# Feed-forward of an encoder trunk: eight of 22 gate/up pairs by seven block products, in a written order

## The chip, the cores and the metric

The kernel runs on one core of a Trainium2 chip. The metric is the device time of one execution in microseconds (us). TensorE multiplies, VectorE, ScalarE and POOL (GpSimd) work on tiles in SBUF, SP issues the transfers, and each engine takes its instructions in the order in which they stand in the program.

## The reference, cut to what matters

```python
D_MODEL, SEQ, DEPTH, D_FF = 1024, 512, 2, 2816          # everything float32

def swiglu(x, w_in, w_out):
    gate, up = jnp.split(x @ w_in, 2, axis=-1)
    return (jax.nn.silu(gate) * up) @ w_out

def reference(x, ffn_w_in, ffn_w_out, ln_g, ln_b, ...):
    for i in range(DEPTH):
        x = layer_norm(DN_ALPHA * x + 0.5 * swiglu(x, ffn_w_in[i, 0], ffn_w_out[i, 0]), ln_g[i, 0], ln_b[i, 0])
        m = neighbourhood_attention(x, ...) if i == 0 else rwkv7_bidir(x, ...)
        x = layer_norm(DN_ALPHA * x + m, ln_g[i, 1], ln_b[i, 1])
        x = layer_norm(DN_ALPHA * x + 0.5 * swiglu(x, ffn_w_in[i, 1], ffn_w_out[i, 1]), ln_g[i, 2], ln_b[i, 2])
    return x
```

There are four feed-forwards (`swiglu`), two in each layer. The change lies in them; the two token mixers stay as they are.

## The kernel before

Tokens: 512. D = 1024 is eight chunks of 128 rows, FF = 2816 is 22 blocks f of 128 columns. TensorE works in a float32 form with a short mantissa, so every operand is split in a high part (`split`, line 276, a copy on ScalarE) and a low part (line 277, raw minus high, on POOL or VectorE), and every product is three matmuls, high·high, high·low and low·high (`mm3`, lines 286 to 288).

`ffn()` runs in 11 steps c of two blocks f. For each f it loads the gate's and the up's weights (two tiles of 128x1024, 512 KB each, `load_cols`), splits them (low on POOL), and multiplies each with the tokens: 24 matmuls of 512 columns into one PSUM bank. Silu of the gate (ScalarE, L491) times the up product (VectorE, L493) gives a 128x512 block, which is stored as two token halves, so that each step has four quarter blocks (2 blocks by 2 halves) of 256.

The product with `w_out` is made by a seven-product scheme of its own (class `Winograd`), with the products X, Y, Z, V and, after the steps, a second Y and so on. `sums(c)` loads 1 MB of `w_out` (tile `ra`), makes sums of its four blocks, stores two of them in DRAM (`d_late`) and splits three (`wx`). Lines 498 to 501 make the sums on the token side; three of the seven quarter tiles are split in `an` and used at once, four in a ring tile (`keep`) for later. `early(c)` is 18 matmuls for X, Y and Z of step c (`product`, L923), issued one step later, so that a step has 96 + 18 = 114 matmuls. X, Y and Z hold six of the eight PSUM banks.

After the steps comes the tail: `add("V", ...)` loads weights in pairs of steps c, splits them (low half on POOL and on VectorE in turn) and multiplies them with the kept halves; `early(10)` stands in its midst; then twelve updates `more` (L520: x ← x + bank, on VectorE) empty the banks of X, Y and Z, and Y, Z and Y again follow with weights from `d_late` and `w_out`, the layer norm, and the next stage's first products (`lead`).

The order on the engines is a planner's: it places instructions by their dependences and by priorities. Inside `manual_schedule` the order in the code holds.

Of the kernel before, what the change touches and what calls it, by code (L numbers as in the profile page):

```python
# [10 lines left out]
F32 = mybir.dt.float32  # L11
# [7 lines left out]
P = 128  # L19
# [62 lines left out]
GN_EPS = 64e-5  # L82

# [22 lines left out]
class Trunk:  # L106
# [161 lines left out]
    def load_cols(self, w, c0, ring=False):  # L268
        return self.load_unit(w[c0 // P], None, ring)
# [191 lines left out]
    def ffn(self, xT, w_in, w_out, ln, nxt, lead=None):  # L461
# [8 lines left out]
        params = ln and self.ln_params(ln)  # L470
        out = Winograd(self, w_out)
        with self.pool("fa") as pool:
            out.pool = pool
            keep = [self.ring().rearrange("p (i n s) -> p i n s", i=2, n=4) for _ in range(npairs)]
            for c in range(npairs):
                if c == 2 and not params:
                    with self.behind(self.asked):
                        params = self.ln_params(ln)
                with self.behind(*() if c or ln else (self.asked,)):
                    out.sums(c)  # L480
                raw = pool.tile([P, 8, 256], F32, name="ar", tag="ar", bufs=1)
                for j in range(2):
                    f = 2 * c + j
                    if f == 0:
                        pps = self.follow()
                    elif not pps:
                        us = self.units if f == 1 else [self.load_cols(w_in, FF * i + f * P) for i in range(2)]
                        pps = [self.proj_cols(u, xT) for u in us]
                    pg, pu = pps.pop(0), pps.pop(0)
                    s = self.tmp()  # L490
                    nc.scalar.activation(s, pg, AF.Silu)  # L491

                    nc.vector.scalar_tensor_tensor(raw[:, 3:7:3] if j else raw[:, 0:8:7], halves_of(pu), 0.5, halves_of(s),  # L493
                                                   ALU.mult, ALU.mult)
                    if j == 0 and c:
                        out.early(c - 1)
                a = lambda n: raw[:, n]
                nc.vector.tensor_tensor(a(1), a(7), a(6), ALU.add)
                nc.vector.tensor_tensor(a(2), a(1), a(0), ALU.subtract)  # L499
                nc.gpsimd.tensor_tensor(a(4), a(0), a(7), ALU.subtract)  # L500
                nc.gpsimd.tensor_tensor(a(5), a(3), a(2), ALU.subtract)
                out.now[c] = pool.tile([P, 2, 3, 256], F32R, name="an", tag="an", bufs=1)
                self.split(out.now[c][:, 0], out.now[c][:, 1], raw[:, 0:3])
                self.split(keep[c][:, 0], keep[c][:, 1], raw[:, 3:7])
            out.keep = keep
# [3 lines left out]
            out.early(npairs - 1)  # L509
            out.add("V", 0, out.b21, range(late, npairs))  # L510
        nxt = nxt()
        with self.pool("fo") as pool:
            out.pool = pool
            out.begin(out.t3)
            fin = self.residual_norm(params, nxt)
# [20 lines left out]
            out.add("Y", 1, out.t3, range(npairs))  # L536
# [3 lines left out]
            out.add("Z", 2, out.b22, range(npairs), lag=8)  # L540
# [337 lines left out]

class Winograd:
# [8 lines left out]
    def sums(self, c):  # L888
# [3 lines left out]
        nc.sync.dma_start(r.rearrange("p j l f -> p j (l f)"), self.w[:, c])  # L892
        t3 = self.pool.tile([P, 512], F32, name="ts", tag="ts", bufs=1)
# [4 lines left out]
        nc.sync.dma_start(self.late[:, 0, c], t3)  # L898
# [1007 lines left out]
```

## Time and profile before

| | |
|---|---|
| time, median of 3 runs | 2162.34 us (2162.04 to 2162.39) |
| the profiled execution: time, span | 2161.41 us, 2159.6 us |
| clock granted to TensorE, mean | 0.999 of full speed |
| busy, share of the span: TensorE, VectorE, ScalarE, POOL | 99%, 49%, 44%, 65% |
| moved by DMA | 322 MB, 149 GB/s |
| the four feed-forwards, from the span's start | about 18 to 355, 600 to 950, 950 to 1290, 1800 to 2155 us |

The rows of the trace say: start, duration, engine, line, operation, tiles out<-in, shape, and in brackets the idle time ahead and what ended it. Groups say: count, busy time in all, mean ns of one, idle time ahead and what ended it. A chain row says start, duration, and what TensorE or a transfer did. A matmul's duration is modelled with its way through the array; what it costs in a stream is the distance of the starts.

### The profile page before, as it was taken

The page shows a single profiled execution, that of the slowest core. Times are in us where ns is not written, and L with a number is a line of the kernel's source. Part 1 is how long each engine was busy: PE and PEld are TensorE (multiplying, and loading weights), DVE is VectorE, ACT ScalarE, POOL GpSimd, SP SyncE. Part 2 cuts the span into 40 slices and gives each one's busy share as a digit, 9 for nine tenths or more (in the row PEclk, how much of TensorE's full clock was granted, in tenths as well). Part 3 has the DMA queues.
Part 4 walks back from the last instruction along what each step waited for, and adds up shares of the span by engine and source line. Part 5 has one row for each costly group of instructions (what it writes and reads, how often), then busy time and mean ns, then how long its engine had stood idle before and what let it go on. Part 6 is the DMA issues. An engine that isn't in the chain of part 4 may idle for free.

```text
span 2159.6 us, 35350 instructions
## 1 busy us (share of the span) xinstructions
PE 2134.2 (99%) x13952; PEld 1684.7 (78%) x13952; DVE 1059.7 (49%) x1526; ACT 954.2 (44%) x1675; POOL 1395.3 (65%) x1226
## 2 busy tenths in 40 slices
PE   9999999999999999999999999999999999999998
PEld 8888888888788888888888888445777558888876
DVE  3233355277333333653333369735998554333345
ACT  4333345367433333443333343636888433333333
POOL 5978855465378888568888653044788615877753
PEclk9999999999999999999999999999999999999999
DMA  7444462342244444634444543864454552444443
GB/s 214 150 152 140 148 230 93 113 122 84 88 156 142 141 142 142 224 132 137 142 141 142 188 143 123 284 223 123 124 138 130 177 190 92 143 141 142 137 165 127
DMA packets 146518, 322.00 MB, mean 149 GB/s; under 512 B 31184, under 2 KB 51280, under 8 KB 146352
## 3 DMA queue, kind: packets, MB, share of 16 engines
q1 hardware_dynamic: 146352, 319.74, 45.4%
q8 instruction: 110, 1.80, 0.4%
q14 instruction: 56, 0.46, 0.1%
HBM read 262.01 MB, written 45.61 MB: 142 GB/s over the span
## 4 chain that ended last, share of the span: by engine, by line
PE 94%; DVE 2%; DMA 1%; ACT 1%; issue 1%; SPq 0%; POOL 0%; DVEq 0%; ACTq 0%; POOLq 0%
PE bank L923 18%; PE bank L287 17%; PE bank L286 17%; PE bank L288 17%; PE a L1115 5%; PE bank L349 4%; PE g L1441 2%; PE y L1115 1%; PE bank L1308 1%; PE m L1115 1%; PE bank L677 1%; PE y L1618 1%; PE c L1611 1%; PE g L1115 1%; PE y L1641 1%
## 5 line engine op out<-in xcount | busy, mean ns | idle before, releaser
L277 POOL TENSOR_TENSOR w<-raw,w 128x1024 fp32r<-128x1024 f32 x198 | 484.6, 2449 | 228.5 <-ACT w L276 221.0
L286 PE MATMUL bank<-xT,w 128*128 128x512 f32 x1264 | 493.4, 390 | 0.0
L287 PE MATMUL bank<-xT,w 128*128 128x512 f32 x1264 | 492.3, 389 | 0.0
L288 PE MATMUL bank<-xT,w 128*128 128x512 f32 x1264 | 491.8, 389 | 0.0
L276 ACT ACTIVATE w<-raw 128x1024 fp32r<-128x1024 f32 x202 | 213.0, 1058 | 321.5 <-POOL ts L894 131.0
L493 DVE SCALAR_TENSOR_TENSOR ar<-bank,tmp 128x512 f32<-128x512 f32 x88 | 60.9, 692 | 572.1 <-PE bank L288 562.1
L288 PEld LDWEIGHTS bank<-xT,w 128*128 128x128 f32 x1264 | 237.3, 188 | 49.4
L286 PEld LDWEIGHTS bank<-xT,w 128*128 128x128 f32 x1264 | 237.3, 188 | 48.7
L287 PEld LDWEIGHTS bank<-xT,w 128*128 128x128 f32 x1264 | 237.4, 188 | 48.6
L923 PE MATMUL bank<-wx,an 128*128 128x512 f32 x792 | 187.5, 389 | 0.0
L923 PEld LDWEIGHTS bank<-wx,an 128*128 128x128 f32 x792 | 148.7, 188 | 31.2
L923 PE MATMUL bank<-w,ring 128*128 128x512 f32 x720 | 168.5, 390 | 1.7 <-POOL w L277 1.7
L277 POOL TENSOR_TENSOR wx<-ra,wx 128x512 fp32r<-128x512 f32 x132 | 167.0, 1292 | 3.2 <-ACT wx L276 3.2
L277 DVE TENSOR_TENSOR ring<-ar,ring 128x1024 fp32r<-128x1024 f32 x44 | 126.0, 2864 | 81.0 <-ACT ring L276 81.0
L923 PEld LDWEIGHTS bank<-w,ring 128*128 128x128 f32 x720 | 135.1, 188 | 30.6 <-POOL w L277 2.2
L491 ACT ACTIVATE tmp<-bank 128x512 f32<-128x512 f32 x88 | 52.6, 597 | 231.7 <-PE bank L288 231.6
L1550 POOL TENSOR_TENSOR tm<-qs,zs 128x126 f32<-128x126 f32 (+22 forms) x248 | 108.8, 439 | 62.8 <-DVE qs L1543 24.6
L1552 POOL TENSOR_TENSOR zs<-zs,tm 128x126 f32<-128x126 f32 (+22 forms) x248 | 109.0, 440 | 19.4
L276 ACT ACTIVATE wx<-ra 128x512 fp32r<-128x512 f32 x132 | 82.8, 633 | 77.0 <-PE bank L923 66.6
L277 POOL TENSOR_TENSOR ring<-raw,ring 128x1024 fp32r<-128x1024 f32 x24 | 59.9, 2508 | 74.8 <-ACT ring L276 74.8
L499 DVE TENSOR_TENSOR ar<-ar 128x256 f32<-128x256 f32 x44 | 92.5, 2102 | 1.5
L277 POOL TENSOR_TENSOR w<-xT,w 128x1024 fp32r<-128x1024 f32 x25 | 63.4, 2538 | 42.2 <-ACT w L276 42.2
(346 smaller groups left out, 3943.1 us busy)
## 6 DMA issues: line engine op xcount, KB each, us to landing
raw<-in_ffn_w_in_dram SPq DMA_DIRECT2D x176, 512.0 KB, 3.5
ra<-in_ffn_w_out_dram SPq DMA_DIRECT2D x44, 1024.0 KB, 5.0
xT<-d_late SPq DMA_DIRECT2D x29, 512.0 KB, 5.3
xT<-in_ffn_w_out_dram SPq DMA_DIRECT2D x23, 512.0 KB, 4.5
d_late<-ts SPq DMA_DIRECT2D x44, 256.0 KB, 3.0
d_late<-ra SPq DMA_DIRECT2D x44, 256.0 KB, 2.0
raw<-in_w_qkv_dram SPq DMA_DIRECT2D x16, 512.0 KB, 3.6
raw<-in_ffn_w_out_dram SPq DMA_DIRECT2D x12, 512.0 KB, 3.6
```

Source lines behind the costliest of these rows:

```text
L276: self.hi = self.nc.scalar.activation(h, raw, AF.Copy).ins
L277: self.lo = (eng or self.nc.vector).tensor_tensor(l, raw, h.bitcast(F32), ALU.subtract).ins
L286: nc.tensor.matmul(out, wh, xh, start=start, stop=False)
L287: nc.tensor.matmul(out, wh, xl, start=False, stop=False)
L288: nc.tensor.matmul(out, wl, xh, start=False, stop=stop)
L349: nc.tensor.matmul(acc[t, h], a, u[:, i, h * 512 : (h + 1) * 512], start=first and n == 0, stop=last and n == 2)
L493: nc.vector.scalar_tensor_tensor(raw[:, 3:7:3] if j else raw[:, 0:8:7], halves_of(pu), 0.5, halves_of(s), ALU.mult, ALU.mult)
L499: nc.vector.tensor_tensor(a(2), a(1), a(0), ALU.subtract)
L923: self.nc.tensor.matmul(acc, lhs, u[:, i], start=bool(first) and m == 0, stop=last and m == 2, skip_group_check=more)
L1115: self.nc.tensor.matmul(out[hs], w[:, hs], x, start=start, stop=stop)
L1550: nc.gpsimd.tensor_tensor(tv, qs[:, s, 0:s].rearrange("p (a o) -> p a o", o=1).broadcast_to([P, s, n]), zs[:, s : s + 1, c0:].broadcast_to ...
L1552: nc.gpsimd.tensor_tensor(zs[:, 0:s, c0:], zs[:, 0:s, c0:], tv, ALU.add)
```

## The change

For odd f from 7 to 21 (`SEVEN`, eight of 22, one in each step from the fourth, called a slot below) gate and up together are made as a 2x2 block product in the manner of Strassen and Winograd: rows gate and up, inner dimension in two halves of 512, tokens in two halves of 256. That takes seven products of 4 chunks x 3 = 12 matmuls of 256 columns (84) in place of 48 of 512 columns. The even f of those steps stay plain, with weights as half tiles.

- Weights come in half tiles of 128x512 (256 KB each). Four of them are turned into sums in place on VectorE (L1034, L1035, L1038, L1042), and eleven are split per slot; `weights()` is the thread that does so. L1042 is the last reader of the first raw half tile, which the next load then fills.
- The token side's four mixed tiles (128x1024) are made once per feed-forward, in the first two steps (`mixes`, L949 to L955, on VectorE).
- Only two PSUM banks serve a slot: the seven products are gathered through copies on ScalarE (L1076) and sums on VectorE (L1099, L1103, L1105, L1109).
- The order on TensorE, ScalarE and VectorE in slots is the string `FF_SEQ`: g is the plain f, s the seven products, e the 18 matmuls of the step before, w the weights, k the work behind the step before (`posts`), z and u the sums and splits of `w_out`.
- Weight splits of the plain blocks, the four sums on `ra`, and all the token sums move from POOL to VectorE.
- Of `keep`, two of four quarter tiles per step go to DRAM (`d_away`) and are read back for Z and the second Y (`recall`). The load of the norm's parameters stands behind the first Y.
- The first two weights of V are loaded and split inside the last slot (`opening`).

What stands in rows, at three places. In names of tiles the number is a running one; `w`, `wl2` are split weights, `xT_...` with a raw weight in it is a buffer that serves for loads in the tail, `ring` in the tail the kept halves, `bank` PSUM, `x0` to `x3` the residual.

First the tail of the first feed-forward. VectorE before: `w_2187` and `w_2237` are weights of V, the first updates follow.

```order
L277 TENSOR_TENSOR w_2187<-xT_2131,w_2187 128x1024 [waits DMAHW7_49,Activation_49]
L277 TENSOR_TENSOR ring_268<-ar_1977,ring_268 128x1024 [waits Activation_49]
L277 TENSOR_TENSOR w_2237<-xT_2132,w_2237 128x512 [waits DMAHW5_49,Activation_49]
L520 SCALAR_TENSOR_TENSOR x0_88<-x0_88,bank_491 128x512 [waits PE_49]
L520 SCALAR_TENSOR_TENSOR x1_89<-x1_89,bank_492 128x512 [waits DMAHW1_49,PE_49]
L520 SCALAR_TENSOR_TENSOR x2_90<-x2_90,bank_499 128x512 [waits DMAHW4_49,PE_49]
L520 SCALAR_TENSOR_TENSOR x0_88<-x0_88,bank_483 128x512 [waits DVE_49]
```

VectorE after: the same place; nine more updates stand ahead of the first row, `w_2718` is V's weight of c = 6 and 7, `w_2768` that of c = 10.

```order
L554 SCALAR_TENSOR_TENSOR x3_91<-x3_91,bank_499 128x512 [waits DVE_49]
L554 SCALAR_TENSOR_TENSOR x3_91<-x3_91,bank_499 128x512
L554 SCALAR_TENSOR_TENSOR x1_89<-x1_89,bank_499 128x512
L280 TENSOR_TENSOR wl2_2788<-xT_2673,wl2_2788 128x1024 [waits DMAHW4_49,DMAHW0_49,Activation_49]
L280 TENSOR_TENSOR w_2718<-xT_2672,w_2718 128x1024 [waits Activation_49]
L280 TENSOR_TENSOR w_2768<-xT_2673,w_2768 128x512 [waits DMAHW6_49,Activation_49]
```

The splits of V's weights on VectorE, which stood ahead of the updates, stand behind all twelve of them, and behind that of `wl2`, a weight of the Y sum.

TensorE there before: `wx`·`an` are products of `early(10)`, `w`·`ring` those of V (c = 6 and 7 by `w_2187`).

```order
L923 MATMUL bank_2133<-w_2187,ring_264 128x512 [waits Activation_49]
L923 MATMUL bank_2134<-w_2187,ring_264 128x512
L923 MATMUL bank_2133<-w_2187,ring_264 128x512 [waits DVE_49]
L923 MATMUL bank_2133<-w_2187,ring_264 128x512
L923 MATMUL bank_2134<-w_2187,ring_264 128x512 x2
L923 MATMUL bank_483<-wx_1968,an_2126 128x512
L923 MATMUL bank_484<-wx_1968,an_2126 128x512
L923 MATMUL bank_491<-wx_1971,an_2126 128x512
L923 MATMUL bank_492<-wx_1971,an_2126 128x512
L923 MATMUL bank_499<-wx_1974,an_2126 128x512
L923 MATMUL bank_500<-wx_1974,an_2126 128x512 x3
```

TensorE after: the end of `early(10)`, then c = 4 and 5 (`w_2702`), then c = 6 and 7 (`w_2718`).

```order
L1200 MATMUL bank_514<-wx_2655,an_2662 128x512
L1200 MATMUL bank_515<-wx_2655,an_2662 128x512
L1200 MATMUL bank_2674<-w_2702,ring_1317 128x512 [waits Activation_49]
L1200 MATMUL bank_2675<-w_2702,ring_1317 128x512
L1200 MATMUL bank_2674<-w_2702,ring_1317 128x512 [waits Pool_49]
L1200 MATMUL bank_2674<-w_2702,ring_1317 128x512
L1200 MATMUL bank_2675<-w_2702,ring_1317 128x512 x2
L1200 MATMUL bank_2674<-w_2702,ring_1317 128x512 x3
L1200 MATMUL bank_2675<-w_2702,ring_1317 128x512 x3
L1200 MATMUL bank_2674<-w_2718,ring_1788 128x512 [waits Activation_49]
L1200 MATMUL bank_2675<-w_2718,ring_1788 128x512
L1200 MATMUL bank_2674<-w_2718,ring_1788 128x512 [waits DVE_49]
```

`early(10)` ended behind the wait for `w_2187`'s low half (the third row), with c = 4 and 5 ahead of it; now it ends ahead of c = 4, and the low halves of `w_2702` (POOL) and then of `w_2718` (VectorE, the last row) are waited for behind it.

Second the first steps. VectorE before, between the products of f = 1 and f = 2 of the first feed-forward (L493 is Silu times up):

```order
L493 SCALAR_TENSOR_TENSOR ar_287<-bank_364,tmp_389 128x2x256 [waits PE_49,Activation_49]
L498 TENSOR_TENSOR ar_287<-ar_287 128x256 [waits DVE_49]
L499 TENSOR_TENSOR ar_287<-ar_287 128x256 [waits DVE_49]
L277 TENSOR_TENSOR an_396<-ar_287,an_396 128x768 [waits Activation_49]
L277 TENSOR_TENSOR ring_258<-ar_287,ring_258 128x1024 [waits Activation_49]
L493 SCALAR_TENSOR_TENSOR ar_419<-bank_455,tmp_480 128x2x256 [waits DVE_49,PE_49]
```

VectorE after, the last 12 of the 20 rows between the same two products (L517 is now Silu times up; `ring_335` holds mixed tokens, `w_528`, `w_621` are weights of f = 3 and f = 4):

```order
L1130 TENSOR_TENSOR ra_412<-ra_412 128x512 [waits DMAHW6_49,DVE_49]
L280 TENSOR_TENSOR w_528<-raw_527,w_528 128x1024 [waits DMAHW0_49,PE_49,Activation_49]
L949 TENSOR_TENSOR ring_335<-xT_93,xT_92 128x1024 [waits DVE_49]
L526 TENSOR_TENSOR ar_283<-ar_283 128x256 [waits DVE_49]
L1133 TENSOR_TENSOR ra_412<-ra_412 128x512 [waits DVE_49]
L280 TENSOR_TENSOR an_402<-ar_283,an_402 128x768 [waits Activation_49]
L951 TENSOR_TENSOR ring_335<-ring_335 128x1024 [waits DVE_49]
L280 TENSOR_TENSOR w_621<-raw_620,w_621 128x1024 [waits DMAHW1_49,Activation_49]
L1134 TENSOR_TENSOR ra_412<-ra_412 128x512 [waits DVE_49]
L280 TENSOR_TENSOR away_408<-ar_283,away_408 128x2x256 [waits Activation_49]
L280 TENSOR_TENSOR ring_258<-ring_335,ring_258 128x1024 [waits Activation_49]
L517 SCALAR_TENSOR_TENSOR ar_430<-bank_442,tmp_491 128x2x256 [waits DVE_49]
```

Splits of weights, sums of `ra` and the mixing of tokens are now on VectorE ahead of the row that empties the bank of f = 2.

Third a slot. VectorE before: a whole step, in the same feed-forward.

```order
L493 SCALAR_TENSOR_TENSOR ar_773<-bank_809,tmp_834 128x2x256 [waits DVE_49,PE_49]
L493 SCALAR_TENSOR_TENSOR ar_773<-bank_890,tmp_915 128x2x256 [waits PE_49,Activation_49]
L498 TENSOR_TENSOR ar_773<-ar_773 128x256 [waits DVE_49]
L499 TENSOR_TENSOR ar_773<-ar_773 128x256 [waits DVE_49]
L277 TENSOR_TENSOR an_922<-ar_773,an_922 128x768 [waits Activation_49]
L277 TENSOR_TENSOR ring_261<-ar_773,ring_261 128x1024 [waits Activation_49]
```

VectorE after: 12 of the 34 rows of a slot, from L1103, which needs the sixth of the seven products, on.

```order
L1103 TENSOR_TENSOR tmp_877<-bank_441,tmp_877 128x256 [waits PE_49]
L1105 SCALAR_TENSOR_TENSOR ar_805<-tmp_877,tmp_876 128x256 [waits Activation_49]
L523 TENSOR_TENSOR ar_805<-ar_805 128x256 [waits DVE_49]
L280 TENSOR_TENSOR ring_261<-raw_774,ring_261 128x512 [waits DMAHW3_49,Activation_49]
L524 TENSOR_TENSOR ar_805<-ar_805 128x256 [waits DVE_49]
L525 TENSOR_TENSOR ar_805<-ar_805 128x256
L1034 TENSOR_TENSOR raw_774<-raw_774 128x512 [waits DMAHW2_49,DVE_49]
L1035 TENSOR_TENSOR raw_774<-raw_774,raw_775 128x512 [waits DMAHW5_49,DVE_49]
L280 TENSOR_TENSOR w_818<-raw_774,w_818 128x512 [waits Activation_49]
L1109 SCALAR_TENSOR_TENSOR ar_805<-bank_442,tmp_876 128x256 [waits PE_49]
L1038 TENSOR_TENSOR raw_774<-raw_775,raw_774 128x512 [waits DVE_49]
L526 TENSOR_TENSOR ar_805<-ar_805 128x256 [waits DVE_49]
```

Where six rows filled a step, 34 do, and the sums of weights (L1034 on) and the splits stand between the rows that TensorE's banks wait for.

The diff, cut to its core:

```diff
+SEVEN = range(7, NF, 2)
+FF_SEQ = ("g k w g w w k g w k z u g k w g s w s w s e e e s w s s u s s u s s u s e s w s e e w u")
...
+        seven = Seven(self, xT, w_in)
         with self.pool("fa") as pool:
             out.pool = pool
-            keep = [self.ring().rearrange("p (i n s) -> p i n s", i=2, n=4) for _ in range(npairs)]
+            keep = []
+            posts = iter(())
             for c in range(npairs):
-                if c == 2 and not params:
-                    with self.behind(self.asked):
-                        params = self.ln_params(ln)
+                if 2 * c + 1 in SEVEN:
+                    with self.tc.manual_schedule(engines=MANUAL_SCAN):
+                        raw = seven.slot(c, out, pool, posts)
+                        posts = self.posts(c, raw, out, seven, keep, pool)
+                        if c == npairs - 1:
+                            list(posts)
+                    continue
...
+                        us = self.units if f == 1 else [self.load_cols(w_in, FF * i + f * P, eng=nc.vector) for i in range(2)]
+                        pps = [self.proj(u, pp, xT) for u, pp in zip(us, seven.banks(f))]
+                    self.gated(pps.pop(0), pps.pop(0), raw[:, 3:7:3] if j else raw[:, 0:8:7])
+                    if f < 4:
+                        seven.mixes(f)
+                    if c and j == 0:
+                        list(out.early(c - 1))
...
+            list(out.early(npairs - 1))
...
+        nc.vector.tensor_tensor(a(4), a(0), a(7), ALU.subtract)
+        nc.vector.tensor_tensor(a(5), a(3), a(2), ALU.subtract)
...
+        away = self.home(self.sb).tile([P, 2, 2, 256], F32R, name="away", tag=("gbc", "bbc")[c % 2])
+        self.split(away[:, :, 0], away[:, :, 1], raw[:, 5:7])
+        nc.sync.dma_start(self.away[:, :, c], away.bitcast(F32).rearrange("p n i s -> p n (i s)"))
...
+            out.add("Y", 1, out.t3, range(npairs), back=out.recall(2))
+            params = self.ln_params(ln)
+            fin = self.residual_norm(params, nxt)
...
+            out.add("Z", 2, out.b22, range(npairs), lag=8, back=out.recall(3))
...
+        def difference(out, t, a, b):
+            tt(out, part_of(a, 0), part_of(b, 0), sub)
+            tt(t, part_of(a, 1), part_of(b, 1), sub)
+            tt(out, out, t, add)
+        def fold(out, a, t):
+            tt(out, part_of(a, 0), t, sub)
+            tt(out, out, part_of(a, 1), add)
...
+        if part == 0:
+            difference(x, y, self.block(0, 1), self.block(0, 0))
+            keep(0, x)
...
+    def slot(self, c, out, pool, posts):
+        if 2 * c + 3 not in SEVEN:
+            self.work = chain(self.work, out.opening())
+        raw = pool.tile([P, 8, 256], F32, name="ar", tag="ar", bufs=1)
+        threads = dict(g=self.plain(2 * c, raw[:, 0:8:7]), s=self.products(2 * c + 1, raw[:, 3:7:3]), e=out.early(c - 1),
+                       w=self.work, k=posts, z=out.third(c - 1), u=out.sums(c, True))
+        for name in FF_SEQ.split():
+            next(threads[name], None)
+        if 2 * c + 3 not in SEVEN:
+            list(out.third(c))
...
+        return raw
...
+        halves = ((0, 0), (0, 1), (1, 0), (1, 1))
+        for ih, raw in zip(halves, r):
+            ask(pairs[0] - 1, *ih, raw)
+        for f in pairs:
+            for raw, ih in zip(r, ((1, 0), (0, 0), (0, 1), (1, 1))):
+                make(raw)
+                ask(f, *ih, raw)
+                yield
+            more = f + 2 in pairs
+            u0, g0, g1, u1 = r
+            make(g0)
+            tt(g0, g0, u0, ALU.subtract)
+            tt(u0, u0, u1, ALU.add)
+            make(u0)
+            yield
+            tt(u0, u1, g0, ALU.subtract)
+            make(u0)
+            yield
+            make(g1)
+            tt(g1, g1, u0, ALU.subtract)
+            if more:
+                ask(f + 1, *halves[0], r[0])
+            yield
+            for n, raw in enumerate((g0, g1, u1)):
+                make(raw)
+                if more:
+                    ask(f + 1, *halves[n + 1], r[n + 1])
+                yield
...
+    def plain(self, f, dst):
+        pps = self.banks(f)
+        for n in range(4):
+            pp = pps[n // 2]
+            self.mul(halves_of(pp), self.units.pop(0), lambda c: self.xT.get(n % 2 * 4 + c), n % 2 == 0, n % 2 == 1)
+            yield
+        self.k.gated(*pps, dst)
+        yield
+    def products(self, f, dst):
+        k, nc = self.k, self.nc
+        a, e = self.banks(f)
+        a, f, e = a[:, :256], a[:, 256:], e[:, :256]
+        s, v, p = k.tmp(), k.tmp(), k.tmp()[:, :256]
+        s, v = halves_of(s), halves_of(v)
+        copy = lambda out, x: nc.scalar.activation(out, x, AF.Copy)
+        b = lambda q, h: lambda c: [self.block(q, h)[:, j, c] for j in range(2)]
+        t = lambda n: lambda c: [self.right[n][:, j, c] for j in range(2)]
+        mul = lambda out, x, start=False: self.mul(out, self.units.pop(0), x, start, True)
+        tt, stt = nc.vector.tensor_tensor, nc.vector.scalar_tensor_tensor
+        mul(a, b(0, 0), True)
+        yield
+        mul(f, t(0))
+        yield
+        copy(e, a)
+        copy(p, f)
+        yield
+        mul(e, t(1))
+        yield
+        copy(v[:, 0], e)
+        yield
+        mul(a, b(1, 0))
+        yield
+        nc.scalar.activation(s[:, 0], a, AF.Silu)
+        yield
+        mul(e, t(2))
+        yield
+        copy(v[:, 1], e)
+        tt(v[:, 1], v[:, 1], p, ALU.add)
+        yield
+        mul(f, b(1, 1))
+        yield
+        tt(v[:, 0], f, v[:, 0], ALU.add)
+        nc.scalar.activation(s[:, 1], v[:, 0], AF.Silu)
+        stt(dst[:, 1], v[:, 1], 0.5, s[:, 1], ALU.mult, ALU.mult)
+        yield
+        mul(e, t(3))
+        yield
+        stt(dst[:, 0], e, 0.5, s[:, 0], ALU.mult, ALU.mult)
+        yield
...
-        nc.gpsimd.tensor_tensor(t3, r[:, 1, 1], r[:, 0, 1], ALU.subtract)
-        nc.gpsimd.tensor_tensor(r[:, 0, 1], r[:, 0, 1], r[:, 0, 0], ALU.subtract)
-        nc.gpsimd.tensor_tensor(r[:, 1, 1], r[:, 1, 1], r[:, 0, 1], ALU.subtract)
-        nc.gpsimd.tensor_tensor(r[:, 1, 0], r[:, 1, 0], r[:, 1, 1], ALU.subtract)
+        nc.vector.tensor_tensor(t3, r[:, 1, 1], r[:, 0, 1], ALU.subtract)
+        nc.vector.tensor_tensor(r[:, 0, 1], r[:, 0, 1], r[:, 0, 0], ALU.subtract)
         nc.sync.dma_start(self.late[:, 0, c], t3)
+        yield
+        nc.vector.tensor_tensor(r[:, 1, 1], r[:, 1, 1], r[:, 0, 1], ALU.subtract)
+        nc.vector.tensor_tensor(r[:, 1, 0], r[:, 1, 0], r[:, 1, 1], ALU.subtract)
...
+    def opening(self):
+        k = self.k
+        raws = {}
+        for c in (0, 2):
+            raws[c] = k.raw()
+            k.nc.sync.dma_start(raws[c].rearrange("p (c f) -> p c f", c=2), self.b21(c, 2))
+            self.loads += 1
+            yield
...
+            k.split(u[:, 0], u[:, 1], raws[c])
...
+    def recall(self, n):
+        self.keep[n] = []
+        for i in range(3):
...
+            self.nc.sync.dma_start(r[:, :m].bitcast(F32), self.k.away[:, n - 2, 4 * i : 4 * i + m])
```

More of the change, by code (lines that the diff above doesn't have):

```diff
@@ L1 @@
 import math
+from itertools import chain
 from contextlib import ExitStack, contextmanager
@@ L486, in ffn @@
                     elif not pps:
[L487 to L505, printed above, removed]
+                        us = self.units if f == 1 else [self.load_cols(w_in, FF * i + f * P, eng=nc.vector) for i in range(2)]
[5 more added lines that the diff above has]
+                        list(out.early(c - 1))
+                list(self.posts(c, raw, out, seven, keep, pool))
+                if 2 * c + 3 in SEVEN:
+                    seven.prepare()
+            out.keep = {n: [k[:, n] for k in keep] for n in range(2)}
             late = npairs - 4
@@ L959, in begin, with add @@
             self.begun[src.__name__, c] = self.load(src, c, False)
-    def add(self, name, n, src, cs, lag=None):
+    def add(self, name, n, src, cs, lag=None, back=()):
         first = self.banks(name)
-        step = lambda c, t: self.product(self.acc[name][t], self.keep[c], n, t, us[c], first and c == 0, c == NF // 2 - 1, name != "V")
+        step = lambda c, t: self.product(self.acc[name][t], self.keep[n][c], t, us[c], first and c == 0, c == NF // 2 - 1, name != "V")
         us = {}
@@ L968, in add @@
                 now = (src.__name__, c)
+                next(iter(back), None)
                 self.duo = self.begun.pop(now) if now in self.begun else self.load(src, c, lag is not None and c >= lag)
```

144 lines of the change are left out of this document (128 added, 16 removed).

## The prediction

> **What bounds the kernel now.** I read the page first (busy shares and chain), then TensorE's waits, then the chain in order of time, and last a table by stretch. The page's lines on engines and chain, the core's span, TensorE's two longest waits in total, the chain's rows at step boundaries, and one feed-forward step as a stretch (busy us and count of each engine):
>
> ```profile
> core 0: 2159.6 us, clock 0.999
> PE 2134.2 (99%) x13952; PEld 1684.7 (78%) x13952; DVE 1059.7 (49%) x1526; ACT 954.2 (44%) x1675; POOL 1395.3 (65%) x1226
> PE 94%; DVE 2%; DMA 1%; ACT 1%; issue 1%; SPq 0%; POOL 0%; DVEq 0%; ACTq 0%; POOLq 0%
> ...
> PE bank L1091 <- DVE ring L1075: 2.6, 3, 1.2
> PE bank L923 <- POOL w L277: 1.7, 1, 1.7
> ...
> 46.46 4.08 PE bank L923 x18
> 72.30 4.08 PE bank L923 x18
> 293.98 58.48 PE bank L923 x258
> 1832.45 4.10 PE bank L923 x18
> 1858.69 4.10 PE bank L923 x18
> ...
> 72.30:98.14 25.84, 25.84 (x115) 21.40 (x115) 6.75 (x6) 9.03 (x11) 23.07 (x15) 1.00 0.45 153
> ```
>
> TensorE is the bound: 99% busy at full clock, and of its waits only one, of 1.7 us, lies in the feed-forward (L923). A step is 114 matmuls of 512 columns back to back: 72.30 − 46.46 = 25.84 us, 0.2267 each; in the fourth feed-forward 1858.69 − 1832.45 = 26.24, 0.2302 each. In such a step POOL is busy 23.07 us and VectorE 6.75. The tail is one unbroken piece (293.98, 258 matmuls, 58.48 us). So anything that TensorE need not do counts in full, and every new wait of TensorE counts in full too.
>
> **Term 1, fewer products: −27 us.** For 8 of the 22 f, 48 matmuls of 512 columns become 84 of 256. The trace has such a run of 256-wide ones, in the lead into the second feed-forward (TensorE's timeline, first and last row of it):
>
> ```profile
> 595.19 0.28 PE L287 MATMUL bank<-xT,ring 128*128 128x256 f32 x1
> ...
> 600.59 0.28 PE L288 MATMUL bank<-xT,ring 128*128 128x256 f32 x1
> ```
>
> That is 45 starts in 5.40 us, 0.120 each. So 84 × 0.120 = 10.08 for 48 × 0.2267 = 10.88: 0.80 us a slot (a step with seven products), and 0.97 in the fourth feed-forward (48 × 0.2302 = 11.05). 24 × 0.80 + 8 × 0.97 = 27 us. An eighth fewer columns gives only 7% less time, because 0.120 is more than half of 0.2267. Bounds: half of it, 0.1133, would save 18 more (2688 × 0.0067); 0.125 would give 13 back. I take 0.120, the same shape in the same kernel.
>
> The Trainium skill has a rule that speaks against the change: "TensorE: Matmul & The Clock Gate", section "Back-to-back issue gap", puts the sustained spacing of pairs of weight load and matmul at about 81 ns for 128 columns and 131 for 512; drawn as a line, my estimate for 256 is 98, and 84 × 98 against 48 × 131 would be 1.9 us a slot lost, +62 in all. This trace does not have that spacing: 227 and 120 stand in its place, and so the rule gets no chance below.
>
> **Term 2, the tail: +24 us.** Rows for VectorE and POOL here (timeline, then groups):
>
> ```profile
> 293.81 6.06 PE L923 MATMUL bank<-w,ring 128*128 128x512 f32 x26
> 299.71 2.43 PE L923 MATMUL bank<-wx,an 128*128 128x512 f32 x10
> 301.97 3.79 PE L923 MATMUL bank<-w,ring 128*128 128x512 f32 x16
> 305.60 1.98 PE L923 MATMUL bank<-wx,an 128*128 128x512 f32 x8
> ...
> 305.15 1.53 DVE L277 TENSOR_TENSOR w<-xT,w 128x512 fp32r<-128x512 f32 x1 [3.28 <-ACT w L276]
> 306.60 5.46 DVE L520 SCALAR_TENSOR_TENSOR x<-x,bank 128x512 f32<-128x512 f32 x9
> 317.49 2.95 DVE L277 TENSOR_TENSOR w<-xT,w 128x1024 fp32r<-128x1024 f32 x1
> 344.20 1.23 DVE L277 TENSOR_TENSOR wl<-rw,wl 128x1024 fp32r<-128x1024 f32 x1
> ...
> L277 POOL TENSOR_TENSOR w<-raw,w 128x1024 fp32r<-128x1024 f32 x198 | 484.6, 2449 | 228.5 <-ACT w L276 221.0
> ```
>
> Before, the low halves of V's last weights that VectorE makes (the last at 305.15) stand ahead of the updates of x (L520, from 306.60, 0.607 each), so TensorE goes on. In the changed order all twelve updates (L554) stand ahead of the low halves of wl2 and of V's pair c = 6, 7, in each of the four feed-forwards. The first update waits for TensorE's end of Y in the last step. From that end VectorE needs 12 × 0.607 + 2 × 1.23 = 9.74 us, and 0.1 for the hand-overs; TensorE has 17 matmuls (three of Y and Z, twelve on c = 4, 5, two on the high half of c = 6, 7) × 0.2267 = 3.85 until the one that needs that low half. It waits 6.0 us, four times: +24. Nothing stands behind to win it back, since the tail was unbroken. Bounds: if the lows run beside POOL, 2.95 for 1.23 as at 317.49, 8 to 9 each, +36; if VectorE's updates start some 2 us ahead of my count, +16. POOL's own low half of c = 4, 5 (2.4 us) and the thirteenth load of that stretch, which it needs, may be late by 1 to 5 us, but that wait lies inside the same 6.
>
> **Term 3, the first three steps: +6 us.** POOL's work goes to VectorE at once, and the token sides are mixed there too (tiles of 1024). Prices with POOL at rest, and beside it:
>
> ```profile
> 1331.36 0.69 DVE L699 TENSOR_TENSOR xT<-tmp,xT 128x512 fp32r<-128x512 f32 x1
> 1331.97 0.69 DVE L693 SCALAR_TENSOR_TENSOR ring<-ring,xraw 128x512 f32<-128x512 f32 x1
> 621.48 0.42 DVE L498 TENSOR_TENSOR ar<-ar 128x256 f32<-128x256 f32 x1
> ...
> L277 DVE TENSOR_TENSOR ring<-ar,ring 128x1024 fp32r<-128x1024 f32 x44 | 126.0, 2864 | 81.0 <-ACT ring L276 81.0
> L499 DVE TENSOR_TENSOR ar<-ar 128x256 f32<-128x256 f32 x44 | 92.5, 2102 | 1.5
> L277 DVE TENSOR_TENSOR an<-ar,an 128x768 fp32r<-128x768 f32 x44 | 57.5, 1307 | 40.2 <-ACT an L276 40.2
> ```
>
> Beside a busy POOL the same form takes twice as long and more (2864 for 1230, 2102 for 420). POOL is nearly empty in these steps afterwards, so I price by the clean rows. Between the product of f = 1 and the one of f = 2 VectorE's order then has nine tiles of 1024 (11.1 us), eight of 512 (5.5), three of 256 (1.3) and one of 768 (about 1.0): 18.9 us, and waits on ScalarE's high halves among them. TensorE wants the bank back after 90 matmuls, 20.4 us. That is 1.5 us of room, with waits on four weight loads in line; I make it 0.6 to 1.7 us late, 1.5 a feed-forward, 6 in all. Bounds: 0 and 12.
>
> **Term 4, the slots: +5 us.** Per slot VectorE has 25 instructions of 512 (0.61 back to back, 0.69 alone), eight of 256 and one of 768: 15.3 to 17.3 + 3.4 + 1.0 = 20 to 22 us of 25.04. That is 80 to 87%, and one chain closes on itself:
>
> ```profile
> raw<-in_ffn_w_in_dram SPq DMA_DIRECT2D x176, 512.0 KB, 3.5
> d_late<-ra SPq DMA_DIRECT2D x44, 256.0 KB, 2.0
> ...
> 125.37 0.63 ACT L276 ACTIVATE wx<-ra 128x512 fp32r<-128x512 f32 x1 [0.25 <-PE bank L923]
> 133.53 0.60 ACT L491 ACTIVATE tmp<-bank 128x512 f32<-128x512 f32 x1 [4.81 <-PE bank L288]
> ```
>
> When the sixth product ends, L1103 may run; from it to L1042, which frees the first raw half tile, stand fifteen VectorE instructions (7 × 0.42 + 8 × 0.65 = 8.1, and one Silu and the seventh product between, 9.0 to 10). Then a 256 KB load (2.6, between 2.0 and 3.5), its high half on ScalarE (0.63) and, behind it there, the Silu of the gate (0.60), which frees the bank that the next slot's first product writes: 13 to 15 us. TensorE has 12 × 0.12 + 9 × 0.2267 + 48 × 0.2267 = 14.36 until then. The slip is 0 to 0.6 on most slots, I take 0.16: 32 × 0.16 = +5. Bounds: 0 and 38 (1.2 each). Cover is thin: every 0.1 us that a slot's load or VectorE chain is longer costs 3.2 us.
>
> **What I cost at nothing.** The half of keep that goes to d_away: 0.5 MB more written a step on SP's queue, 4.0 MB where there were 3.5, against a DMA share of 0.45 in the step quoted; the six reads back stand a pair or more ahead of the Z and Y products. ScalarE's copies of banks: with sixteen of 512 at 0.63 and a few small ones it is about 13 us busy of 25. The load of the norm's parameters, moved behind the first Y sum, still has the 66 matmuls of Z (15 us) ahead of its use. If the cover of the reads goes (VectorE late at the tail), Z's first pair waits, 1 to 3 us a feed-forward.
>
> **The sum.** −27 + 24 + 6 + 5 = +8 us, with 1 for the reads: +9 on the profiled execution (span 2159.6, 2161.41 in all, 0.9 below the median 2162.34): 2170.4, and for the median 2171.
>
> **Rivals.** (a) Slots and first steps hide all they got: −27 + 24 = −3, 2159. For: 80 to 87% leaves 3 us a slot. Against: the chain of 13 to 15 against 14.36. (b) The slots run on VectorE's chain, not on TensorE: at a slip of 0.8 they win nothing; 32 × 0.64 more, 2191. For: fifteen instructions in line and a load inside the loop. Against: the room of 3 to 5 us on VectorE. (c) The other side: VectorE is through the updates before TensorE needs the low half, because V's products that I count behind them give it longer; the tail then costs nothing, 2147, and half, 2159. It decides where the tail costs under 3 us each. Against: twelve updates in one line, each 0.607, all behind an end that TensorE sets. (d) 256-wide products at half the pitch: 2153; it decides below 0.115. Against: 45 starts at 0.120. That the products aren't made in seven blocks is excluded by the order of instructions.
>
> **How the numbers follow.** A measurement of this kernel can tell about 0.2%, 4.3 us, from no change: 2158.0 to 2166.7. Forecast 0.40 (its own range 2163 to 2180), (a) 0.22, (b) 0.20, (c) 0.14, (d) 0.04. Faster: (c), (d) and a little of (a), 0.20. Same: most of (a) and the low end of the forecast, 0.25. Slower: the rest, 0.55. The range from 2150 to 2195 leaves out the lower half of (c) and the worst of (b), under 0.2.
>
> **What would show it.** TensorE's waits after: four of about 6 us on L1200 for the low half w (L280) on VectorE; waits of 0.5 to 3 us on L289 for L517 in steps 1 and 2; slots of 25.0 to 25.4 us; 256-wide starts at 0.120 on L1056; VectorE's tiles of 512 at 0.6 to 0.7. Slots over 25.8, or 256-wide starts off 0.120, or no wait in the tail, make it wrong.

## The result, and the profile after

The changed kernel takes 2207.8 us (median of 4, 2204.11 to 2212.44), before 2162.19 (4 runs): a ratio of 1.0214 (95%: 1.0202 to 1.0227), 46 us slower. The forecast was 2171, range 2150 to 2195, slower at 0.55: the sign was right, the size was not.

The page and the span line of the changed kernel, and TensorE's waits in it (waits of the line named, total us, times, longest):

```profile
core 0: 2202.3 us, clock 0.988
PE 2130.1 (97%) x15104; PEld 1724.3 (78%) x15104; DVE 1548.6 (70%) x2634; ACT 1087.3 (49%) x2119; POOL 513.4 (23%) x666
PE 69%; DVE 13%; DMA 11%; ACT 3%; issue 3%; POOL 0%; SPq 0%; ACTq 0%; DVEq 0%; POOLq 0%
...
PE bank L1200 <- ACT w L279: 20.9, 5, 5.7
PE bank L1056 <- ACT tmp L516: 15.8, 14, 3.1
PE bank L1200 <- POOL w L280: 5.4, 4, 1.7
PE bank L1200 <- DVE w L280: 2.8, 4, 0.8
...
PE bank L289 <- DVE ar L517: 2.5, 4, 0.7
```

TensorE was 94% of the chain and is 69% now, with 11% transfers and 13% VectorE in its place. Three things to see: the longest waits of L1200 (the tail) are for ScalarE's *high* half of a weight, not for VectorE's low half as forecast; L516, the Silu of a plain gate, is waited for 14 times; and the mean clock fell from 0.999 to 0.988, which a step-by-step sum of waits does not contain.

To place the loss, I cut each feed-forward at four starts of TensorE's timeline that both kernels have: the last transposes on entry, the first matmul of the fourth step, V's first matmul, and the last transposes behind the tail (for the fourth, the first of the last 30 matmuls of L923 or L1200). Before against after, in us:

| feed-forward | first three steps | eight steps or slots | tail |
|---|---|---|---|
| 1 | 72.01 → 72.85 | 206.72 → 205.92 | 78.10 → 88.32 |
| 2 | 64.85 → 65.76 | 206.72 → 206.81 | 78.10 → 88.03 |
| 3 | 64.85 → 65.76 | 206.72 → 207.35 | 70.62 → 81.55 |
| 4 | 65.46 → 66.34 | 209.89 → 207.82 | 59.65 → 69.28 |
| sum of differences | +3.5 | −2.1 | +40.7 |

That is +42.1 of the 42.7 between the two profiled executions (2204.11 and 2161.41). The tails carry nearly all of it, and the slots, which by terms 1 and 4 should have given 22, gave 2.

**The tail.** The first one in TensorE's timeline, then the links of the chain in it, VectorE's part, and four short stretches with the granted clock (the number ahead of the DMA share):

```profile
300.38 4.24 PE L1200 MATMUL bank<-wx,an 128*128 128x512 f32 x18
309.68 1.22 PE L1200 MATMUL bank<-w,ring 128*128 128x512 f32 x2 [5.07 <-ACT w L279]
312.13 13.78 PE L1200 MATMUL bank<-w,ring 128*128 128x512 f32 x52 [1.23 <-POOL w L280]
325.75 2.88 PE L1200 MATMUL bank<-wl,ring 128*128 128x512 f32 x12
...
298.35 10.20 DMA raw<-in_ffn_w_out_dram
309.71 2.38 POOL w L280
...
303.97 7.26 DVE L554 SCALAR_TENSOR_TENSOR x<-x,bank 128x512 f32<-128x512 f32 x12 [2.50 <-PE bank L1200]
313.09 3.40 DVE L280 TENSOR_TENSOR w<-xT,w 128x1024 fp32r<-128x1024 f32 x1
...
304.00:309.60 5.60, 0.62 (x3) 0.19 (x1) 5.60 (x10) 2.08 (x3) 0.00 (x0) 0.89 1.04 411
309.60:311.00 1.40, 1.22 (x2) 0.50 (x2) 1.40 (x3) 1.40 (x3) 1.29 (x1) 0.50 1.04 418
313.00:314.00 1.00, 1.00 (x3) 0.72 (x3) 1.00 (x2) 0.00 (x0) 1.00 (x1) 0.50 1.00 401
316.00:317.00 1.00, 1.00 (x5) 0.54 (x4) 0.65 (x2) 0.63 (x1) 0.00 (x0) 1.00 1.03 358
```

When `early(10)` ends, the weight of c = 4, 5 is not there: its load was issued only at 298.35 and took 10.20 us, with a DMA share of 1.04 (411 GB/s). TensorE waits 5.07 for its high half and 1.23 for POOL's low half. Then it runs at half clock to about 315: the 52 matmuls from 312.13 take 13.62 us to the next row, 1.8 more than at 0.2267. VectorE's twelve updates and the low half of c = 6, 7 (303.97 to 316.49) run beside all this. TensorE's first matmul with that low half heads this row:

```profile
316.54 1.66 PE L1200 MATMUL bank<-w,ring 128*128 128x512 f32 x6
```

So the load is what TensorE waits for, and the order that I had put at the centre comes due just as TensorE gets there. By the starts of single matmuls it costs 0.16 us in this tail, and in the other three the low half is ready 0.7 to 0.95 us ahead of its use. The order is hidden, but with next to no room.

**A slot.** The first slot: TensorE's row, ScalarE's two rows ahead of it, and the links of the chain that lead there; then the same wait in the second feed-forward, with the clock behind it, and a later slot's part:

```profile
101.58 1.69 PE L1056 MATMUL bank<-xT,ring 128*128 128x256 f32 x12 [2.73 <-ACT tmp L516]
...
100.42 0.63 ACT L279 ACTIVATE w<-raw 128x512 fp32r<-128x512 f32 x1 [2.65 <-DMA raw<-in_ffn_w_in_dram]
100.95 0.58 ACT L516 ACTIVATE tmp<-bank 128x512 f32<-128x512 f32 x1
...
95.81 0.69 DVE raw L1042
97.73 2.58 DMA raw<-in_ffn_w_in_dram
...
697.00 2.59 PE L1056 MATMUL bank<-xT,ring 128*128 128x256 f32 x12 [2.92 <-ACT tmp L516]
...
698.00:699.00 1.00, 1.00 (x7) 1.00 (x7) 0.39 (x1) 0.00 (x0) 0.00 (x0) 0.50 0.58 193
...
104.72 2.07 PE bank L1200 x9
113.23 1.43 PE bank L1056 x12
129.80 2.07 PE bank L1200 x9
```

This is the chain of my term 4, link by link: L1042, a load of 2.58 us, its high half, and behind that in ScalarE's queue the Silu. Where nothing waits a slot takes 129.80 − 104.72 = 25.08 us (forecast 25.04) and twelve 256-wide matmuls 1.43 (0.119 each).

### The profile page after: what moved, and what is told of

Same layout as the page of the kernel before. It is cut to its first block, busy times and chain, and to the rows that moved or that the text cites. A ratio compares the mean times of both kernels' runs of the same rounds, so it can differ in the third digit from the quotient of the medians.

```text
span 2202.3 us, 39167 instructions
## 1 busy us (share of the span) xinstructions
PE 2130.1 (97%) x15104; PEld 1724.3 (78%) x15104; DVE 1548.6 (70%) x2634; ACT 1087.3 (49%) x2119; POOL 513.4 (23%) x666
## 4 chain that ended last, share of the span: by engine, by line
PE 69%; DVE 13%; DMA 11%; ACT 3%; issue 3%; POOL 0%; SPq 0%; ACTq 0%; DVEq 0%; POOLq 0%
PE bank L1200 14%; PE bank L1056 14%; PE bank L290 5%; PE bank L289 5%; PE bank L291 5%; DMA ra<-in_ffn_w_out_dram 5%; PE a L1393 5%; PE bank L352 4%; DMA raw<-in_ffn_w_out_dram 2%; DVE w L280 2%; DMA raw<-in_ffn_w_in_dram 2%; PE g L1719 2%; DVE ring L280 2%; DVE wx L280 1%; PE y L1393 1%
## 5 line engine op out<-in xcount | busy, mean ns | idle before, releaser
L280 POOL TENSOR_TENSOR w<-raw,w 128x1024 fp32r<-128x1024 f32 x34 | 83.5, 2461 | 1249.8 <-ACT w L279 1239.8
L279 ACT ACTIVATE w<-raw 128x512 fp32r<-128x512 f32 (+1 forms) x306 | 221.6, 732 | 252.9 <-DVE raw L1034 47.7
L1056 PE MATMUL bank<-xT,w 128*128 128x512 f32 (+1 forms) x1476 | 280.7, 344 | 4.5 <-ACT tmp L516 4.3
L1056 PEld LDWEIGHTS bank<-xT,w 128*128 128x128 f32 x1476 | 238.0, 189 | 43.0 <-ACT tmp L516 9.4
L280 DVE TENSOR_TENSOR w<-raw,w 128x512 fp32r<-128x512 f32 (+1 forms) x272 | 205.5, 765 | 64.0 <-ACT w L279 62.8
L1200 PE MATMUL bank<-w,ring 128*128 128x512 f32 x720 | 181.1, 409 | 29.2 <-ACT w L279 20.9
L1200 PE MATMUL bank<-wx,an 128*128 128x512 f32 x792 | 199.9, 392 | 0.0
L1200 PEld LDWEIGHTS bank<-w,ring 128*128 128x128 f32 x720 | 141.1, 198 | 66.5 <-ACT w L279 24.0
L1056 PE MATMUL bank<-xT,ring 128*128 128x512 f32 (+1 forms) x828 | 162.4, 350 | 11.6 <-ACT tmp L516 11.6
L1056 PEld LDWEIGHTS bank<-xT,ring 128*128 128x128 f32 x828 | 136.4, 190 | 34.8 <-ACT tmp L516 14.6
L1200 PEld LDWEIGHTS bank<-wx,an 128*128 128x128 f32 x792 | 142.9, 189 | 24.9
L289 PE MATMUL bank<-xT,w 128*128 128x512 f32 x368 | 145.1, 394 | 2.5 <-DVE ar L517 2.5
L290 PE MATMUL bank<-xT,w 128*128 128x512 f32 x368 | 143.5, 390 | 0.0
L291 PE MATMUL bank<-xT,w 128*128 128x512 f32 x368 | 142.9, 390 | 0.0
L1056 PE MATMUL bank<-ring,w 128*128 128x256 f32 x1056 | 140.6, 283 | 0.0
L1056 PEld LDWEIGHTS bank<-ring,w 128*128 128x128 f32 x1056 | 135.5, 191 | 3.6
L280 DVE TENSOR_TENSOR wx<-ra,wx 128x512 fp32r<-128x512 f32 x132 | 89.0, 685 | 11.3 <-ACT wx L279 10.4
```

The costliest lines, as they stand in the source:

```text
L279: self.hi = self.nc.scalar.activation(h, raw, AF.Copy).ins
L280: self.lo = (eng or self.nc.vector).tensor_tensor(l, raw, h.bitcast(F32), ALU.subtract).ins
L289: nc.tensor.matmul(out, wh, xh, start=start, stop=False)
L290: nc.tensor.matmul(out, wh, xl, start=False, stop=False)
L291: nc.tensor.matmul(out, wl, xh, start=False, stop=stop)
L1056: self.nc.tensor.matmul(out, w[:, i, cs], x(c)[j], start=start and c + n == 0, stop=stop and c == 3 and n == 2, skip_group_check=True)
```

## The experiments

Theories before the runs: **L**, the tail is lost to one load that is issued late and lands slowly, and the clock falls behind that wait; **O**, the forecast's, the order on VectorE; **S**, slots are lost to the Silu's place on ScalarE; and their rivals, as quoted.

**The third load early.** `raw` has few buffers, and the last slot holds them; a spare tile is free.

```diff
-        if self.loads < 3:
+        if self.loads < 2:
             raw = k.raw()
         elif self.raws:
```

> One number is changed in load(): the third pair of V's weights (c = 4, 5) goes into a free part of the pair of spare tiles instead of the third `raw` tile, so it need not wait for the last slot's raw tiles. In the instruction order the planner then also puts the low half of c = 6, 7 ahead of the twelve updates. Theory L (the tail loses about 10 us because that one load is issued late, lands after 10 us in a full queue, and TensorE then runs some microseconds at a lower granted clock): each tail 10 us shorter, about 40 in all, near 2165; no wait of TensorE for a high half of w in the tail, clock back to 0.995 or more. Theory Q (the tail is bound by transfers at 400 GB/s whatever the order): at most 2 us a tail, near 2200, the wait moves to another load. Prologue and slots as in the changed kernel.

Measured: 2163.17 us (10 runs), ratio to before 1.0005 (0.9996 to 1.0015): 44.6 us gone. TensorE's first tail and its remaining waits:

```profile
304.48 1.52 PE L1200 MATMUL bank<-wx,an 128*128 128x512 f32 x6
306.75 2.88 PE L1200 MATMUL bank<-wx,an 128*128 128x512 f32 x12
309.47 8.32 PE L1200 MATMUL bank<-w,ring 128*128 128x512 f32 x36
...
PE bank L1056 <- ACT tmp L516: 12.0, 9, 3.6
PE bank L1200 <- DVE w L280: 2.2, 3, 0.8
```

No wait for a high half over 0.2 us is left, the clock is 0.997, and the tails take 80.03, 79.22, 71.56 and 58.73. Theory L's forecast came true, and Q falls: the tails are 37.6 us shorter in sum than the changed kernel's. This run moves the low half of c = 6, 7 ahead of the updates too, so it does not part L from O; the next two change one of them each.

**V's low halves on POOL, the load left late.**

```diff
-        k.split(u[:, 0], u[:, 1], raw, k.nc.vector if c % 4 else k.nc.gpsimd)
+        k.split(u[:, 0], u[:, 1], raw, k.nc.vector if c % 4 and src != self.b21 else k.nc.gpsimd)
```

> The low halves of V's weights loaded in the tail are all made on POOL, so that no split of V stands behind VectorE's twelve updates; the third load stays where it was. Theory O (my prediction's: the tail waits because the low half of c = 6, 7 stands behind the updates): TensorE's waits in the tail go from 7 to 1 us, 24 us in all, near 2183. Theory L: the wait of 5 us for the high half of c = 4, 5 and of 1.2 for its low half stay, the clock is low behind them, and the time stays within 6 us of the changed kernel's (2202 to 2212).

Measured: 2197.88 us, ratio 1.016 (1.0145 to 1.0175). The waits in the tail are as they were:

```profile
PE bank L1200 <- ACT w L279: 20.2, 5, 5.7
PE bank L1200 <- POOL w L280: 4.9, 4, 1.2
```

The tails (88.45, 87.90, 80.58, 67.43) are 2.8 us shorter in sum than the changed kernel's. Another 4.0 us in the profile lie in slots that this edit does not touch, and the time is 4 us below what L allowed, so L's range was missed on the low side. O's 24 us are not there: with the load late, the order was not what TensorE waited for.

**The load early, the order kept late.** The updates are written ahead of V's second half, and the low half of c = 6, 7 is queued behind the last of them (`hold`); the load is early as in the first run.

```diff
...
+        if src == self.b21 and c == 6:
+            k.nc.scalar.activation(u[:, 0], raw, AF.Copy)
+            with k.behind(self.hold):
+                k.nc.vector.tensor_tensor(u[:, 1], raw, u[:, 0].bitcast(F32), ALU.subtract)
+            return u
...
```

> The third load early as in e1, and the low half of c = 6, 7 held behind all twelve updates on VectorE (issued after the last of them). TensorE has seven matmuls of X, Y, Z left when the updates start and needs that low half next. Theory O's price for an order of this kind: 12 x 0.607 + 2 x 1.23 - 7 x 0.227 + 0.1 = 8.3 us a tail, 33 us more than e1, and a low clock behind it on top, 2 to 4 us a tail. If the order is harmless (rival): as e1.

Measured: 2210.27 us, ratio 1.0212 (1.0195 to 1.0229), 47 us over the first run. The wait, and the clock in it and behind it:

```profile
PE bank L1208 <- DVE w L1242: 40.1, 4, 10.9
...
316.00:319.00 3.00, 0.00 (x0) 0.00 (x0) 3.00 (x5) 0.72 (x1) 0.00 (x0) 0.51 1.03 408
322.00:325.00 3.00, 2.75 (x7) 2.17 (x8) 1.33 (x2) 0.00 (x0) 0.00 (x0) 0.50 1.06 412
325.00:328.00 3.00, 3.00 (x12) 2.40 (x11) 0.00 (x0) 1.06 (x1) 0.10 (x1) 0.78 1.00 392
```

So an order of that kind does cost: 10.0 us a tail where 8.3 were worked out (a split for c = 10, 2.50 us at 310.25, stands ahead of the updates too), and the tails are 12.35, 12.43, 11.19 and 12.09 longer than in the first run, 2 us each on the mean over the wait, which the clock of 0.50 explains. Mechanism O is real; in the changed kernel the load hid it. The three runs together: without the order alone the tails are 2.8 us shorter, with the load early and an order of that kind kept they are 10.4 us longer, and without both they are 37.6 us shorter. A late load, or an order of that kind, is each enough to lose the tail, and the gain of the first run belongs to neither alone.

**The Silu ahead of the splits.** The Silu of the plain gate gets an item of its own in the written order.

```diff
-FF_SEQ = ("g k w g w w k g w k z u g k w g s w s w ...
+FF_SEQ = ("g k w g w w k g w k z u g g k w g s w s w ...
...
-        self.k.gated(*pps, dst)
+        s = self.k.tmp()
+        self.nc.scalar.activation(s, pps[0], AF.Silu)
+        yield
+        self.nc.vector.scalar_tensor_tensor(dst, halves_of(pps[1]), 0.5, halves_of(s), ALU.mult, ALU.mult)
         yield
```

> In the written order ScalarE's Silu of the plain gate stands ahead of the k and w items that follow it (`g g k w g s` for `g k w g s`; its product with the up half keeps its place on VectorE). Theory S (a slot's first product waits because this Silu, which frees its bank, stands behind the high half of a late half tile): the waits on L516, 15.8 us in all, go, and with them the low clock behind the first slot's, together 18 to 22 us: near 2187. Theory W (the weights themselves are what is late, the Silu is only in line with them): the waits move to another instruction of the same slot and the time stays within 5 us.

Measured: 2183.37 us, ratio 1.0099 (1.0078 to 1.0120): 24.4 us less than the changed kernel, a little over the 18 to 22 expected (19.9 between the two profiled executions, 18.8 of it in the slots). The waits for a Silu in slots fall to 0.7 us in all, and the second feed-forward's eight slots, from the first of these rows to the second, take 200.70 us, 25.09 each:

```profile
679.14 7.19 PE L1056 MATMUL bank<-xT,w 128*128 128x512 f32 x31
879.84 0.39 PE L1203 MATMUL bank<-w,ring 128*128 128x512 f32 x1
```

The other three take 201.99, 202.66 and 203.79. Theory S holds; the weights were in time (W falls). Without waits a slot gives what term 1 said.

**The reads of `d_away` behind the load.** The edit is to SP's queue: the first two reads, 1 MB each, are issued behind V's third load (`mark`). The planner's order on VectorE moved with it: the low half of c = 6, 7 stands behind six of the updates, not behind twelve.

```diff
...
-                next(iter(back), None)
+                with self.k.behind(*((self.mark,) if back else ())):
+                    next(iter(back), None)
...
```

> The changed kernel, with the first two reads of d_away (1 MB each) issued behind the third load of V on SP's queue, not ahead of it. Theory R (these reads, which I costed at nothing, are a good part of why that load takes 10 us to land): it lands 4 to 5 us sooner, the wait of 5 us falls to 1 or 2, and with the shorter stretch at a low clock the time is 12 to 24 us less than the changed kernel's. Rival (the load is late by its place and its raw tile; the reads are covered): within 5 us of the changed kernel.

Measured: 2184.29 us, ratio 1.0102 (1.0089 to 1.0115), 23.5 us less than the changed kernel. The load, TensorE's waits, VectorE's split of c = 6, 7, and a stretch with the granted clock:

```profile
295.47 8.36 DMA raw<-in_ffn_w_out_dram
304.96 0.73 PE L1201 MATMUL bank<-w,ring 128*128 128x512 f32 x2 [0.80 <-ACT w L279]
307.41 13.71 PE L1201 MATMUL bank<-w,ring 128*128 128x512 f32 x52 [1.73 <-POOL w L280]
...
307.11 1.33 DVE L280 TENSOR_TENSOR w<-xT,w 128x1024 fp32r<-128x1024 f32 x1
...
309.00:310.00 1.00, 1.00 (x4) 0.81 (x3) 1.00 (x3) 0.00 (x0) 1.00 (x1) 0.50 1.03 418
```

The load is issued 2.9 us sooner and lands 1.8 us faster; the wait for its high half falls from 5.07 to 0.80. The tails (83.75, 83.80, 77.18, 62.85) are 19.6 us shorter in sum, about half of their loss. The theory was right on the sum, though the gain came more from the place in the queue than from the flight. How much of it the shorter order on VectorE gave was not parted from the reads; in the other three tails TensorE now waits 2.2 to 2.4 us for low halves from VectorE, so the order shows as the load's wait shrinks.

A full DMA queue alone is no loss. Two stretches of before, then the first of them in the changed kernel:

```profile
285.00:290.00 5.00, 5.00 (x24) 4.14 (x23) 0.00 (x0) 1.43 (x2) 2.23 (x2) 1.00 0.28 100
300.00:305.00 5.00, 5.00 (x24) 4.14 (x23) 1.87 (x2) 2.01 (x3) 1.27 (x1) 1.00 1.02 395
...
285.00:290.00 5.00, 5.00 (x44) 5.00 (x43) 1.80 (x3) 1.67 (x4) 0.00 (x0) 1.00 1.03 371
```

Before reached a share of 1.02 in its tail too, with TensorE busy throughout, and the first run has 1.03 from 300 to 305 without the loss. What is new is that the transfers fill up ahead of the tail, with the weight that TensorE needs next still to be issued.

**Both mends, and one slot more.** The edits of the first and the fourth run together, and then `SEVEN = range(5, NF, 2)` on top.

> The edits of e1 and of e4 together in the changed kernel. If the two losses are separate (tail 44.6 by e1, slots 24.4 by e4): 2207.8 - 44.6 - 24.4 = 2139, 1% faster than before, slots at 25.09 us each, the clock at 0.998, TensorE's waits in feed-forwards under 1 us each. If they share something (a transfer queue that is full when slots run faster): 2150 or more, with waits back in the tail or the slots.

> As e8, with the seven products for nine f in place of eight (from f = 5, the third step). Term 1's price by the trace of e4 (slots at 25.09 for steps of 25.84, and 26.24 in the fourth feed-forward): 3 x 0.75 + 1.15 = 3.4 us less than e8. Rival (the third step has no room on VectorE, where the mixing of tokens has just ended): the first slot waits, 0 to 10 us more than e8.

Measured: 2147.80 us (2141.24 to 2151.13), ratio 0.9933 (0.9920 to 0.9945), for both mends; 2147.94 us, 0.9932 (0.9920 to 0.9944), with nine slots. The first one's span and its largest wait, in total, on the products with `w_out`, and the wait that came back with nine slots:

```profile
core 0: 2142.2 us, clock 0.998
PE bank L1203 <- DVE w L280: 2.6, 4, 0.8
...
PE bank L1056 <- ACT tmp L1067: 3.1, 6, 1.3
```

By the medians both mends give 60.0 us of the 69.0 that they gave one by one: the time lies between the 2139 of separate losses and the 2150 of shared ones. By the profiled executions they are separate: 40.0 and 19.9 alone, 60.2 together. This is the fastest version, 14.2 us under before; its slots take 24.3 us less than the eight steps did. The ninth slot's 3.4 us did not show: its profile has 3.1 us of waits for the Silu, where eight slots have 0.5. That these waits are the whole reason is not shown.

## Why the prediction was right or wrong

- **Term 1 (−27): right.** Slots without waits take 25.09 us, 256-wide matmuls 0.119, and with both mends the slots of the four feed-forwards give 6.0, 5.5, 5.9 and 6.9, which is 24.3 of the 27. The sustained spacing that the Trainium skill gives in "TensorE: Matmul & The Clock Gate", section "Back-to-back issue gap", did not show in the changed kernel either.
- **Term 2 (+24): mis-sized, 40.7, and its step "that wait lies inside the same 6" failed.** I had seen the thirteenth load and put its lateness at 1 to 5 us inside the wait for VectorE's order. It was the other way round: the load (10.20 us in flight) set the wait, 0.76 + 5.07 + 1.23 in the first tail and about 29 in all four, and the order lay within it; the wait of 6.0 for the low half of c = 6, 7 did not come. That half was itself ready only as TensorE got to it, since the last two splits took 2.01 and 3.40 where I had 1.23 each. Another 1.5 to 2.6 us a tail are TensorE at half clock after the wait, a term that the sum lacked; waits and half clock make about 38 of the 40.7; I had written the bound of +36 for POOL's contention, not for this. That the time went up as forecast is in part luck: the tail lost by another wait than the one that was priced.
- **"What I cost at nothing": wrong for the reads of `d_away`.** I weighed 0.5 MB more a step against a mean DMA share of 0.45. What mattered was the stretch ahead of the tail, where the share went from 0.28 to 1.03, and the load that was still to come in it; with the two reads behind that load, and VectorE's order moved with them, the time is 23.5 us less. I had asked only when the reads were due, not what was queued behind them.
- **Term 3 (+6): 3.5**, with a wait of about 0.6 us on L517 in each feed-forward: right in place, under in size.
- **Term 4 (+5): mis-sized, 25** (27 to be won, 2.1 won); a slot takes 25.87 on the mean, over the 25.8 that the prediction gave as a sign of being wrong. The chain and its links were right. The slip of 0.16 was taken for every slot, but the first slot starts behind the first three steps' backlog on VectorE, and its waits alone are 2.73, 2.92, 3.07 and 1.31, with half clock behind two of them; the last slots lost 0.2 to 1.0 each. The waits sum to 15.8, the half clock behind two of them to some 3.4; what makes the rest was not parted. What the step missed is that the Silu did not have to be in that chain: the order put it there.
- **Rivals.** (b), slots on VectorE's chain, came nearest (2191, with the slots giving nothing), but by luck: the slots lost by the Silu's place on ScalarE, not by VectorE's chain, and the tail was the larger error. (a) and (c) did not come; (d) was excluded by 0.119.

## What to carry to other kernels

Before a transfer is costed at nothing, look at the DMA share of the stretch in which it is issued, and at what stands behind it in its queue: a mean of 0.45 hid a stretch at 1.03 with the weight that was needed next behind it. When two waits could end at nearly the same place, price each as if the other were gone; the one that seems to contain the other may be the one contained, and taking away one alone may give little. And in an order written by hand, put what frees a TensorE bank ahead of any instruction on that engine that waits for a transfer.

## What the runs showed of the hardware that was not expected

After a wait TensorE's granted clock is 0.50 for a time, from inside the wait until some microseconds after the work is back: 308.3 to 315.1 in the first tail, 697.4 to 700.8 behind the wait of 2.92 us, 316.1 to 326.3 with the 10.9 us wait. In each tail of the changed kernel 1.5 to 2.6 us are lost by it, by the starts of the twelve matmuls behind the wait against 0.2267 each. A wait of 2.73 us left the clock at full speed, and one of 2.92 us in the next feed-forward brought it to 0.50; with the reads moved, waits of 0.80 and 1.73 us close together were followed by 0.50 too. The Trainium skill has this in "TensorE: Matmul & The Clock Gate", section "What's actually happening": half of the pulses pass after an idle window of about 3.4 us that runs free of the program. The trace agrees with the 0.50 and with the length, for the three stretches last 6.8, 3.4 and 10.2 us; on the wait that sets it off it differs, since waits shorter than 3.4 us were enough. The clock's share was read from rows and from the difference of two kernels' tails; no run took the low clock away and left the wait.

VectorE's split of 1024 beside a busy POOL took 3.40 us in the tail (1.23 alone), and the twelve updates, which read a bank, 7.26 for twelve, 0.605 each, as before. Runs of the changed kernel and its mended forms spread by 0.2 to 0.5% from their lowest to their highest run, where before spreads by 0.1 to 0.2%; what makes single slots fall out differently was not settled.
